# One product for both halves of the keys' operand in an RWKV-7 mixer, with doubled rates

## The chip, the cores and the metric

The kernel runs on one core of a Trainium2 chip. The metric is device time in microseconds (us) of one execution. The core has five engines that run their own instruction queues in order: TensorE (PE, matmuls; its weight loads are shown as PEld), VectorE (DVE), ScalarE (ACT), GpSimd (POOL) and SyncE (SP, which only issues DMAs here).

## The reference, cut to what matters

The whole program is one layer of a latent-token backbone (1024 latent tokens, 256 context tokens, width 1024): a norm, one input projection, three token mixers side by side (RG-LRU, RWKV-7, S5), a gated merge, a SwiGLU and a last norm. The change touches the RWKV-7 mixer alone. It has 8 heads of 64 channels and runs in both directions `d`:

```
w_log = -softplus(-(w0[d] + tanh(wd[:, :, d]) @ w2[d])) - 0.5
decay = exp(-exp(w_log))                       # = exp(-KAPPA * sigmoid(...)), KAPPA = exp(-0.5)
iclr  = sigmoid(a0[d] + ad[:, :, d] @ a2[d])   # the rate a
k_d   = k * (1 + (iclr - 1) * k_a)
s     = s * w_t - (s @ kk_t) (kk_t * a_t) + v_t k_t          # the state, token by token
y     = s @ r_t ;  bonus = sum(r * k_d * r_k) * v
```

The kernel does the scan in chunks of 32 tokens. Within a chunk the keys' operand is divided by the running product of decays: `kk * iclr / P` and `k_d / P`, where 1/P = exp(KAPPA * cum) and `cum` is the running sum of the decays' sigmoids.

## The kernel before, in words

The channels of the mixer come as four pairs of heads (128 partitions). `run` (line 1819) calls `rwkv_pair(p)` for p = 0 to 3, and then the chain over the 40 chunks, `rwkv_chain`, which goes through both directions side by side and must take one chunk after the other. A pair first makes `kk` (a norm with a reciprocal, lines 743 to 749), then goes through 10 groups of 128 tokens, two of the context and eight latent ones. Each group has three parts, one group apart in the loop at line 870:

- `pre` (765 to 783): PE makes the logits of decays and rates for both directions, 512 columns in one PSUM bank: halves `w = 0` (decays) and `w = 1` (rates). ACT takes tanh(x/2) of all 512 (line 777), DVE makes the sigmoid 0.5 t + 0.5 of all 512 (line 778, "the affine") and then two scans over the decays' half (780, 781) into `cum`.
- `mid` (785 to 828): ACT makes `pf` = P (797) and `pi` = 1/P (798). POOL makes t1 = kk * a (807). ACT makes t2 = ka * a + (1 - ka) (808) and POOL multiplies it by k (809). DVE makes `kr` and, in two products, both halves of `kb`: t1 * pi (811) and t2 * pi (812). For latent groups POOL adds the two directions of t2 into `ks` (818), DVE multiplies by r * r_k (819), and PE sums over the channels (821). DVE and ACT then make the gates `glt` (824 to 826).
- `post` (830 to 889): PE multiplies `kb` with `kr` (843), DVE masks the result to `al` (844), ACT copies the square blocks to `aq` (851), PE transposes `kb` (855), ACT copies that to `kt` (856), and SP stores all of it for the chain.

At the end of a pair `aq` is inverted by 60 small products (`rwkv_inverse`, 909 and 911) between two DVE transposes each at the start and the end (904, 905, 913, 914). For pairs 0 to 2 the products run on POOL, under the next pair's groups; for pair 3 and for the context's blocks `aqc` (the first two groups of all pairs) they run on DVE. `aq` has one buffer, so the next pair's first copy to it waits until the inverse has been stored. The auxiliary PSUM tiles of the stage have five buffers, and an `al` holds one until its `aq` copy is done.

PE is filled between these steps with matmuls of other parts of the program (the input projection, line 1302, and the gates' projection, line 1308); `s.fill` hands them out at fixed places of the loop. The order on each engine is set beforehand, by a scheduler that goes through the program with durations of its own; a change of one instruction can so move others.

Of the kernel before, what the change touches and what calls it, by code (L numbers as in the profile page):

```python
# [16 lines left out]
P = 128  # L17
# [604 lines left out]
KAPPA = math.exp(-0.5)  # L622
# [13 lines left out]
class RwkvMixin:  # L636
# [23 lines left out]
    def rwkv_setup(s, pool):  # L660
        nc = s.nc
# [11 lines left out]
        s.tiny = pool.tile([P, 1], F32, name="tiny", tag="tiny")  # L673
        nc.gpsimd.memset(s.tiny, 1e-12)
        s.ka1 = pool.tile([P, 4], F32, name="ka1", tag="ka1")
        nc.vector.tensor_scalar(s.ka1, s.pv("ka"), -1.0, 1.0, op0=ALU.mult, op1=ALU.add)
        s.aqc = pool.tile([P, 32, 32], F32, name="aqc", tag="aqc")
        s.rk_next = None
        s.pf, s.wdt = [], []
# [47 lines left out]
    def rwkv_pair(s, p, pool):  # L727
        nc = s.nc
# [22 lines left out]
        st = {}  # L751
# [13 lines left out]
        def pre(g):  # L765
            sl = slice(P * g, P * g + P)
            wdt = s.wdt[g % 2]
            nc.sync.dma_start(wdt[0:64].rearrange("l k d t -> l (k d) t"),
                              s.wda_d.rearrange("l k d t -> l (k d) t")[:, :, sl])
            ps = s.aux()  # L770
            for w in range(2):
                for d in range(2):
                    o = 256 * w + P * d
                    nc.tensor.matmul(ps[:, o : o + P], w2a[:, w, d], wdt[:, w, d], start=True, stop=True)
            swa = pool.tile([P, 2, 2, P], F32, name="swa", tag="swa", bufs=2)
            sw = swa.rearrange("p w d t -> p (w d t)")
            S.activation(sw, ps, AF.Tanh, scale=0.5)
            V.tensor_scalar(sw, sw, 0.5, 0.5, op0=ALU.mult, op1=ALU.add)
            cum = pool.tile([P, 2, P], F32, name="cum", tag="cum", bufs=2)
            V.tensor_tensor_scan(cum[:, 0], s.smask, swa[:, 0, 0], 0.0, ALU.mult, ALU.add)  # L780
            V.tensor_tensor_scan(cum[:, 1, ::-1], s.smask, swa[:, 0, 1, ::-1], 0.0, ALU.mult, ALU.add)
            pf = s.pf[g % 2]
            st[g] = [swa, cum, pf]

        def mid(g):
# [9 lines left out]
            bc = lambda x: ch(mb(x[:, sl], 2))  # L795
            pi = pool.tile([P, 2, 4, 32], F32, name="pi", tag="pi", bufs=2)
            S.activation(pcur, ch(cum), AF.Exp, scale=-KAPPA)
            S.activation(pi, ch(cum), AF.Exp, scale=KAPPA)
            G.tensor_scalar(s.pcend[:, 0, p, 4 * g : 4 * g + 4], pm[:, 0, :, 32], 1.0, None, op0=ALU.mult)
            G.tensor_scalar(s.pcend[:, 1, p, 4 * g : 4 * g + 4], pm[:, 1, :, 1], 1.0, None, op0=ALU.mult)  # L800
            a4 = ch(swa[:, 1])
            t1 = pool.tile([P, 2, 4, 32], F32, name="t1", tag="t1", bufs=2)
            t2 = pool.tile([P, 2, 4, 32], F32, name="t2", tag="t2", bufs=2)
            kb = pool.tile([P, 4, 2, 64], F32, name="kb", tag="kb", bufs=2)
            kr = pool.tile([P, 2, 4, nr], F32, name="kr", tag="kr", bufs=2)
            kbv = kb.rearrange("p c d x -> p d c x")
            G.tensor_tensor(t1, bc(kk), a4, op=ALU.mult)
            S.activation(t2, a4, AF.Identity, scale=c1("ka"), bias=s.ka1[:, p : p + 1])
            G.tensor_tensor(t2, t2, bc(k), op=ALU.mult)
            V.tensor_tensor(kr[:, :, :, 0:32], bc(kk), pprev, op=ALU.mult)  # L810
            V.tensor_tensor(kbv[:, :, :, 32:64], t1, pi, op=ALU.mult)
            V.tensor_tensor(kbv[:, :, :, 0:32], t2, pi, op=ALU.mult)
            if lat:
                V.tensor_tensor(kr[:, :, :, 32:64], bc(st["r"]), pcur, op=ALU.mult)
                ks = pool.tile([P, P], F32, name="ks", tag="ks", bufs=2)
                vs = pool.tile([P, P], F32, name="vs", tag="vs", bufs=2)
                k2 = t2.rearrange("p d c t -> p d (c t)")
                G.tensor_tensor(ks, k2[:, 0], k2[:, 1], op=ALU.add)
# [1228 lines left out]
```

## Time and profile before

| | us |
|---|---|
| runs | 2295.26, 2298.51, 2294.9 (median 2295.26) |
| profiled execution | 2292.87 |
| its span, first to last instruction | 2291.1 |
| PE busy | 2071.9 (90%) |
| DVE busy | 1623.8 (71%) |
| POOL busy | 1135.8 (50%) |
| ACT busy | 925.9 (40%) |

The span is the time between the first and the last instruction of the profiled execution, and 1.8 us lie around it. "Busy" is an engine's time in instructions; matmuls are pipelined, so a busy PE need not be at its peak. The four pairs lie between 716 and 1126 us of the span, the chain from 1128 to about 1450. The granted clock is a share of full speed of TensorE.

### The profile page before, as it was taken

Reading aid. Unit: us, or ns where it says so; the run is one execution under the profiler, and the core shown is the slowest. Engines: PE = TensorE matmul, PEld = TensorE weight load, DVE = VectorE, ACT = ScalarE, POOL = GpSimd, SP = SyncE. Lnnn points to the kernel's source line nnn. Section 1 sums busy time; section 2 is a strip of 40 time slices with the busy share of each in tenths; the row PEclk is TensorE's granted clock in tenths of the full one; section 3 lists DMA queues with packets and bytes.
Section 4 is the critical chain, followed back from the end, with each engine's and each line's share of the span. In section 5 each row is a group of like instructions: output and inputs, shape, how many; then the busy total and the mean of one; then the engine's idle time right before and its main releaser. Section 6 shows DMA issues by size and latency. Waiting matters only on the chain. (4 is left out here: it accounts for less than half of the span.)

```text
span 2291.1 us, 38462 instructions
## 1 busy us (share of the span) xinstructions
PE 2071.9 (90%) x14441; PEld 1650.5 (72%) x14441; DVE 1623.8 (71%) x2253; ACT 925.9 (40%) x1740; POOL 1135.8 (50%) x1260
## 2 busy tenths in 40 slices
PE   5989978887899988898599999889799999999998
PEld 3868856565778777786467676668588888887786
DVE  5656698889665787889963346853985666568977
ACT  5314345433343646453533433424533232324453
POOL 3662389954522483948100023343564545437656
PEclk7989989998999999999699999999899999999999
DMA  6634322321662635354877768554132323238334
GB/s 258 169 113 114 96 62 76 96 81 60 138 179 75 188 104 156 98 144 122 240 194 165 181 164 210 158 196 152 61 125 92 115 88 120 97 115 298 113 117 153
DMA packets 371751, 314.08 MB, mean 137 GB/s; under 512 B 67239, under 2 KB 313198, under 8 KB 370542
## 3 DMA queue, kind: packets, MB, share of 16 engines
q1 hardware_dynamic: 369134, 304.28, 45.8%
q10 hardware_dynamic: 1728, 6.29, 0.8%
q8 instruction: 114, 1.87, 0.3%
q0 software_dynamic: 704, 1.05, 0.2%
q14 instruction: 71, 0.58, 0.1%
HBM read 217.20 MB, written 94.35 MB: 136 GB/s over the span
## 5 line engine op out<-in xcount | busy, mean ns | idle before, releaser
L1562 PE MATMUL mm<-q,wt 128*128 128x512 f32 x1584 | 376.5, 398 | 4.8 <-DVE q L1476 3.8
L1562 PEld LDWEIGHTS mm<-q,wt 128*128 128x128 f32 x1584 | 299.5, 189 | 77.6 <-DVE q L1476 4.2
L1302 PE MATMUL mm<-xh,wh 128*128 128x512 f32 (+1 forms) x576 | 215.8, 382 | 8.3 <-ACT ya L180 4.8
L1786 PE MATMUL mm<-wt,hk 128*128 128x512 f32 x924 | 218.3, 398 | 5.0 <-DVE hk L1476 4.1
L1302 PE MATMUL mm<-xl,wh 128*128 128x512 f32 (+1 forms) x576 | 215.9, 382 | 1.2 <-DVE xl L1218 1.2
L1786 PEld LDWEIGHTS mm<-wt,hk 128*128 128x128 f32 x924 | 174.5, 189 | 48.7 <-DVE hk L1476 5.5
L1308 PE MATMUL mm<-xh,zh 128*128 128x512 f32 x384 | 161.9, 422 | 9.9 <-ACT zge L1344 5.8
L1308 PE MATMUL mm<-xl,zh 128*128 128x512 f32 x384 | 160.9, 419 | 0.0
L1302 PE MATMUL mm<-xh,wl 128*128 128x512 f32 (+1 forms) x576 | 140.3, 381 | 6.9 <-DVE wl L1295 6.4
L1302 PEld LDWEIGHTS mm<-xh,wh 128*128 128x128 f32 x576 | 115.1, 200 | 28.7 <-ACT ya L180 5.7
L1302 PEld LDWEIGHTS mm<-xl,wh 128*128 128x128 f32 x576 | 114.8, 199 | 19.5 <-DVE xl L1218 1.5
L1308 PE MATMUL mm<-byt,bwh 128*128 128x512 f32 x384 | 118.7, 428 | 7.5 <-DVE bsg L1375 2.2
L1308 PE MATMUL mm<-xh,zl 128*128 128x512 f32 x384 | 110.3, 424 | 14.7 <-DVE zl L1295 14.7
L1302 PEld LDWEIGHTS mm<-xh,wl 128*128 128x128 f32 x576 | 102.4, 196 | 27.8 <-DVE wl L1295 8.1
L1015 DVE TENSOR_TENSOR x<-cg,pcend 64x256 f32<-64x256 f32 x152 | 63.9, 421 | 78.6 <-PE cg L1011 36.0
L1292 POOL CAST bwh<-bwr 128x512 fp32r<-128x512 f32 x16 | 9.9, 617 | 209.2 <-PE mm L1308 111.8
L1475 ACT ACTIVATE wt<-wT 128x512 fp32r<-128x512 f32 x88 | 55.0, 631 | 141.4 <-PE mm L1562 130.3
L1476 DVE TENSOR_TENSOR hk<-hraw,hk 128x512 fp32r<-128x512 f32 x77 | 89.4, 1169 | 24.5 <-ACT hk L1475 24.5
L1268 DVE SCALAR_TENSOR_TENSOR macc<-wm,cs,macc 128x256 f32<-128x256 f32 x112 | 87.1, 777 | 23.0 <-DMA wm<-in_w_mod_dram 20.8
L1308 PEld LDWEIGHTS mm<-xh,zl 128*128 128x128 f32 x384 | 75.1, 201 | 34.3 <-DVE zl L1295 17.5
L1002 ACT ACTIVATE x<-cu 32x256 f32<-32x256 f32 x156 | 58.6, 376 | 101.1 <-PE cu L998 98.0
L1476 DVE TENSOR_TENSOR wt<-wt 128x512 fp32r<-128x512 f32 x70 | 75.2, 1077 | 32.1 <-ACT wt L1475 31.6
(434 smaller groups left out, 5022.5 us busy)
## 6 DMA issues: line engine op xcount, KB each, us to landing
wt<-in_w_ffn_in_dram SPq DMA_DIRECT2D x44, 512.0 KB
hraw<-hidd SPq DMA_DIRECT2D x77, 256.0 KB
hidd<-ft SPq DMA_DIRECT2D x75, 256.0 KB
wm<-in_w_mod_dram SPq DMA_DIRECT2D x64, 256.0 KB
gyl<-gyl SPq DMA_DIRECT2D x32, 512.0 KB
wr<-in_w_in_dram SPq DMA_DIRECT2D x27, 512.0 KB
zr<-in_w_in_dram SPq DMA_DIRECT2D x24, 512.0 KB
sgd<-zge SPq DMA_DIRECT2D x48, 256.0 KB
```

The costliest lines, as they stand in the source:

```text
L1002: S.activation(st["x"][96:128, :, par, :], ps[o : o + 32, 0:256].rearrange("p (a k) -> p a k", a=4), AF.Copy)
L1015: V.tensor_tensor(xn[0:64, :, par, :], sn[r].rearrange("p (a k) -> p a k", a=4), vb(s.pcend[r, d, :, st["c"]], 64), op=ALU.mult)
L1268: nc.vector.scalar_tensor_tensor(acc, wm[:, j], s.cs[:, k + j, 0:1], acc, op0=ALU.mult, op1=ALU.add)
L1292: s.nc.gpsimd.tensor_copy(hi, raw)
L1302: s.nc.tensor.matmul(ps, w(k), a(k), start=n == 0, stop=n == len(seq) - 1)
L1308: s.nc.tensor.matmul(ps, w[:, k], a[:, k], start=n == 0, stop=n == len(seq) - 1)
L1475: s.nc.scalar.activation(hi, raw, AF.Copy)
L1476: (eng or s.nc.vector).tensor_tensor(lo, raw, hi, op=ALU.subtract)
L1562: nc.tensor.matmul(ps, w[:, k], a[:, k], start=n == 0, stop=n == len(seq) - 1)
L1786: nc.tensor.matmul(banks[c % 2][t], a[:, i, P * t : P * t + P], b[:, j], start=c in (0, 1, 3, 5) and k == 0 and q == 0, stop=c in (1, 3, 5 ...
```

## The change

Everything lies in `rwkv_setup`, `pre` and `mid`. The affine step is done for the decays' half alone. The rates stay as the tanh t, with a = (1 + t)/2, so that what is kept is 2a = t + 1, and the missing half goes into the inverse decay: `pi` = exp(KAPPA * cum - ln 2), a bias from a small constant tile. t1 is now t + 1 by ACT (new line 812), then times kk by POOL in place (813). t2 is ka * t + (2 - ka) by ACT, which is twice the old value, then times k by POOL. Both lie in one tile `t12`, 32 tokens of t2 beside 32 of t1, and one DVE product of 512 elements with `pi` repeated makes both halves of `kb` (817). `ks` is twice its old value, and r_k is halved once in the setup. Three small constants are added there, one by DVE and two by POOL.

```diff
-        nc.vector.tensor_scalar(s.ka1, s.pv("ka"), -1.0, 1.0, op0=ALU.mult, op1=ALU.add)
+        nc.vector.tensor_scalar(s.ka1, s.pv("ka"), -1.0, 2.0, op0=ALU.mult, op1=ALU.add)
+        s.rkh = pool.tile([P, 4], F32, name="rkh", tag="rkh")
+        nc.vector.tensor_scalar(s.rkh, s.pv("rk"), 0.5, None, op0=ALU.mult)
+        s.lnh = pool.tile([P, 1], F32, name="lnh", tag="lnh")
+        nc.gpsimd.memset(s.lnh, -math.log(2.0))
+        s.one = pool.tile([P, 1], F32, name="one", tag="one")
+        nc.gpsimd.memset(s.one, 1.0)
...
-            V.tensor_scalar(sw, sw, 0.5, 0.5, op0=ALU.mult, op1=ALU.add)
+            V.tensor_scalar(sw[:, 0:256], sw[:, 0:256], 0.5, 0.5, op0=ALU.mult, op1=ALU.add)
...
-            S.activation(pi, ch(cum), AF.Exp, scale=KAPPA)
+            S.activation(pi, ch(cum), AF.Exp, scale=KAPPA, bias=s.lnh)
...
-            t1 = pool.tile([P, 2, 4, 32], F32, name="t1", tag="t1", bufs=2)
-            t2 = pool.tile([P, 2, 4, 32], F32, name="t2", tag="t2", bufs=2)
+            t12 = pool.tile([P, 2, 4, 2, 32], F32, name="t12", tag="t12", bufs=2)
+            t2, t1 = t12[:, :, :, 0], t12[:, :, :, 1]
...
-            kbv = kb.rearrange("p c d x -> p d c x")
-            G.tensor_tensor(t1, bc(kk), a4, op=ALU.mult)
+            S.activation(t1, a4, AF.Identity, bias=s.one)
+            G.tensor_tensor(t1, t1, bc(kk), op=ALU.mult)
             S.activation(t2, a4, AF.Identity, scale=c1("ka"), bias=s.ka1[:, p : p + 1])
             G.tensor_tensor(t2, t2, bc(k), op=ALU.mult)
             V.tensor_tensor(kr[:, :, :, 0:32], bc(kk), pprev, op=ALU.mult)
-            V.tensor_tensor(kbv[:, :, :, 32:64], t1, pi, op=ALU.mult)
-            V.tensor_tensor(kbv[:, :, :, 0:32], t2, pi, op=ALU.mult)
+            V.tensor_tensor(kb.rearrange("p c d (w x) -> p d c w x", w=2), t12,
+                            pi.unsqueeze(3).to_broadcast([P, 2, 4, 2, 32]), op=ALU.mult)
...
-                V.scalar_tensor_tensor(ks, st["r"][:, sl], c1("rk"), ks, op0=ALU.mult, op1=ALU.mult)
+                V.scalar_tensor_tensor(ks, st["r"][:, sl], s.rkh[:, p : p + 1], ks, op0=ALU.mult, op1=ALU.mult)
```

The lines of the changed kernel are numbered 5 to 6 higher behind the edits. The scheduler puts other instructions in another order too, on all engines within the stage. Three places follow. A number behind a name tells buffers apart; `nt` is the inverse's work tile.

ACT, pair 3, group 7 of the groups 0 to 9, from its tanh (`swa`) to the copies to `aq` that wait for pair 2's inverse. Before:

```order
L777 ACTIVATE swa_9546<-aux_9541 128x512
L808 ACTIVATE t2_9649<-swa_9546,ka1_5208,pv2_1305 128x256
L826 ACTIVATE glt_9575<-aux_9572,pv2_1305 128x128
L797 ACTIVATE pf1_5215<-cum_9549 128x8x32
L798 ACTIVATE pi_9643<-cum_9549 128x256
L851 ACTIVATE aq_8797<-aux_9322 32x128 x4
L851 ACTIVATE aq_8797<-aux_9419 32x128 x4
L851 ACTIVATE aq_8797<-aux_9506 32x128 x4
```

After, first group 7 again, then, one group later, the copies:

```order
L783 ACTIVATE swa_9516<-aux_9511 128x512
L812 ACTIVATE t12_9617<-swa_9516,one_5214 128x8x32
L814 ACTIVATE t12_9617<-swa_9516,ka1_5208,pv2_1305 128x8x32
L831 ACTIVATE glt_9544<-aux_9541,pv2_1305 128x128
L803 ACTIVATE pf1_5221<-cum_9519 128x8x32
L804 ACTIVATE pi_9612<-cum_9519,lnh_5212 128x256
```

```order
L831 ACTIVATE glt_9634<-aux_9631,pv2_1305 128x128
L856 ACTIVATE aq_8773<-aux_9294 32x128 x4
L856 ACTIVATE aq_8773<-aux_9390 32x128 x4
L856 ACTIVATE aq_8773<-aux_9476 32x128 x4
L856 ACTIVATE aq_8773<-aux_9566 32x128 x4
L856 ACTIVATE aq_8773<-aux_9652 32x128 x4
```

The copies of the latent groups 2 to 4 stood behind group 7; now those of groups 2 to 6 stand behind group 8.

DVE, pair 3, the two transposes that end pair 2's inverse (L913 and L914 before, L918 and L919 after) among the context's inverse. Before:

```order
L811 TENSOR_TENSOR kb_9559<-t1_9557,pi_9552 128x2x4x32
L812 TENSOR_TENSOR kb_9559<-t2_9558,pi_9552 128x2x4x32
L913 STREAM_TRANSPOSE aq_7675<-nt_8708 64x32x32
L914 STREAM_TRANSPOSE aq_7675<-nt_8708 64x32x32
L911 TENSOR_TENSOR nt_9201<-nt_9201 128x18x13
L824 TENSOR_TENSOR vs_9569<-aux_9572,zr_8925 128x128
L909 TENSOR_TENSOR nt_9201<-nt_9201 128x238
L778 TENSOR_SCALAR swa_9546<-swa_9546 128x512
```

After:

```order
L916 TENSOR_TENSOR nt_9174<-nt_9174 128x10x21
L817 TENSOR_TENSOR kb_9618<-t12_9617,pi_9612 128x2x4x64
L918 STREAM_TRANSPOSE aq_7661<-nt_8684 64x32x32
L919 STREAM_TRANSPOSE aq_7661<-nt_8684 64x32x32
L914 TENSOR_TENSOR nt_9174<-nt_9174 128x198
L784 TENSOR_SCALAR swa_9606<-swa_9606 128x256
```

The transposes stood behind group 6's `kb`, with group 7's affine behind them; now they stand behind group 7's `kb`, and the context's inverse is eight of its 30 steps further on.

DVE, pair 3, the two transposes that end the context's inverse (`aqc`). Before, they stand behind the last `kb` and the last `al` of the pair:

```order
L1364 SCALAR_TENSOR_TENSOR byt_10070<-byr_10071,byt_10070 128x512
L909 TENSOR_TENSOR nt_9201<-nt_9201 128x30
L844 TENSOR_TENSOR al_9936<-aux_9937,amask_1317 128x512
L911 TENSOR_TENSOR nt_9201<-nt_9201 128x30
L1364 SCALAR_TENSOR_TENSOR byt_10070<-byr_10075,byt_10070 128x512
L913 STREAM_TRANSPOSE aqc_5210<-nt_9201 64x32x32
L914 STREAM_TRANSPOSE aqc_5210<-nt_9201 64x32x32
```

After, group 9's affine, scans, `kr` and `kb` still follow (`byt` is another branch's work):

```order
L918 STREAM_TRANSPOSE aqc_5216<-nt_9174 64x32x32
L919 STREAM_TRANSPOSE aqc_5216<-nt_9174 64x32x32
L784 TENSOR_SCALAR swa_9692<-swa_9692 128x256
L829 TENSOR_TENSOR vs_9714<-aux_9717,zr_8900 128x128
L1369 SCALAR_TENSOR_TENSOR byt_10036<-byr_10037,byt_10036 128x512
L786 SCALAR_TENSOR_TENSOR cum_9695<-smask_5199,swa_9692 128x128
L787 SCALAR_TENSOR_TENSOR cum_9695<-smask_5199,swa_9692 128x128
L1369 SCALAR_TENSOR_TENSOR byt_10036<-byr_10041,byt_10036 128x512
```

So the context's inverse, which the chain's first steps need, now ends a group earlier on DVE, and the last group comes behind it.

## Rows read from the trace of the kernel before

**Rows 1.** Four pairs: us; busy PE, PEld, DVE, ACT, POOL; clock; DMA share; GB/s.

```profile
716.00:804.00 88.00, 82.61 (x729) 70.57 (x728) 74.21 (x120) 54.78 (x124) 37.64 (x62) 1.00 0.56 153
804.00:912.00 108.00, 93.86 (x742) 78.21 (x741) 85.70 (x122) 52.89 (x121) 71.02 (x122) 0.94 0.49 134
912.00:1020.00 108.00, 99.48 (x779) 84.33 (x778) 92.14 (x126) 55.71 (x124) 72.82 (x125) 0.94 0.47 130
1020.00:1126.00 106.00, 78.32 (x635) 64.65 (x633) 99.84 (x180) 49.83 (x119) 65.97 (x111) 0.88 0.55 152
```

**Rows 2.** Waits, 700 to 1170 us: who for whom, us in total, times, longest.

```profile
ACT t L808 <- DVE swa L778: 68.2, 30, 6.5
POOL t L807 <- DVE swa L778: 64.0, 23, 8.1
...
PE aux L821 <- DVE ks L819: 18.6, 9, 4.3
```

**Rows 3.** Single lines (ns min/median/max), then groups by form (busy us, mean ns).

```profile
L778 DVE TENSOR_SCALAR swa<-swa x40: 363/427/1998, 724.7 to 1105.6; 128x512 f32<-128x512 f32 x40
...
L811 DVE TENSOR_TENSOR kb<-t,pi x40: 409/416/869, 733.9 to 1113.2; 128x256 f32<-128x256 f32 x40
...
L812 DVE TENSOR_TENSOR kb<-t,pi x40: 409/419/2114, 734.2 to 1113.6; 128x256 f32<-128x256 f32 x40
...
L812 DVE TENSOR_TENSOR kb<-t,pi 128x256 f32<-128x256 f32 x40 | 25.5, 638 | 0.0
L808 ACT ACTIVATE t<-swa,ka,pv 128x256 f32<-128x256 f32 x40 | 23.9, 599 | 68.5 <-DVE swa L778 68.2
...
L811 DVE TENSOR_TENSOR kb<-t,pi 128x256 f32<-128x256 f32 x40 | 19.7, 492 | 0.2 <-PE aux L855 0.2
...
L798 ACT ACTIVATE pi<-cum 128x256 f32<-128x256 f32 x40 | 16.0, 401 | 0.0
```

**Rows 4.** Groups by form of the nearest other shapes, whole span (the first: 700 to 1180).

```profile
L844 DVE TENSOR_TENSOR al<-aux,amask 128x512 f32<-128x512 f32 x32 | 21.7, 678 | 3.2 <-DMA gyl<-al 2.8 <-PE aux L843 0.4
...
L1364 DVE SCALAR_TENSOR_TENSOR byt<-byr,byt 128x512 fp32r<-128x512 f32 x20 | 14.6, 743 | 6.0 <-ACT byt L1363 5.8
...
L448 DVE TENSOR_SCALAR s<-s 64x128 f32<-64x128 f32 x16 | 3.7, 231 | 2.9 <-PE aux L453 2.8
...
L153 ACT ACTIVATE gi<-aux,lru_hb 128x256 f32<-128x256 f32 x8 | 3.7, 466 | 0.2 <-PE aux L150 0.2
```

**Rows 5.** Busy time of a stretch of 10 us in pair 2, columns as in rows 1.

```profile
950.00:960.00 10.00, 7.93 (x59) 7.07 (x61) 7.34 (x16) 4.21 (x11) 9.69 (x21) 0.66 0.23 55
```

**Rows 6.** Timelines, pair 3: start us, us, instruction, [idle before, who ended it].

```profile
1086.08 0.60 ACT L777 ACTIVATE swa<-aux 128x512 f32<-128x512 f32 x1 [0.24 <-PE aux L774]
...
1089.37 2.13 DVE L914 STREAM_TRANSPOSE aq<-nt 64x1024 f32<-64x1024 f32 x1
...
1092.36 0.42 DVE L778 TENSOR_SCALAR swa<-swa 128x512 f32<-128x512 f32 x1
...
1092.88 0.60 ACT L808 ACTIVATE t<-swa,ka,pv 128x256 f32<-128x256 f32 x1 [6.20 <-DVE swa L778]
...
1092.86 0.73 POOL L807 TENSOR_TENSOR t<-kk,swa 128x256 f32<-128x256 f32 x1 [6.76 <-DVE swa L778]
...
1093.78 0.66 PE L855 MATMUL aux<-ident,kb 128*128 128x128 f32 x4 [2.18 <-ACT glt L826]
1096.98 2.08 PE L774 MATMUL aux<-wdt,w2a 65*128 65x128 f32 x8 [2.54 <-ACT aq L851]
...
1095.81 3.39 ACT L851 ACTIVATE aq<-aux 32x128 f32<-32x128 f32 x12
```

**Rows 7.** Timelines, start of the chain.

```profile
1123.98 1.96 DVE L914 STREAM_TRANSPOSE aqc<-nt 64x1024 f32<-64x1024 f32 x1
...
1128.49 1.07 PE L985 MATMUL mm<-x,gyc 128*32 128x64 f32 x16 [12.63 <-ACT x L929]
1134.03 1.06 PE L998 MATMUL mm<-gs,tt 32*32 32x64 f32 x16 [4.48 <-DMA tt<-ttd]
```

More of the change, by code (lines that the diff above doesn't have):

```diff
@@ L816, in mid @@
                 vs = pool.tile([P, P], F32, name="vs", tag="vs", bufs=2)
-                k2 = t2.rearrange("p d c t -> p d (c t)")
-                G.tensor_tensor(ks, k2[:, 0], k2[:, 1], op=ALU.add)
-                V.scalar_tensor_tensor(ks, st["r"][:, sl], c1("rk"), ks, op0=ALU.mult, op1=ALU.mult)
+                G.tensor_tensor(ks.rearrange("p (c t) -> p c t", c=4), t2[:, 0], t2[:, 1], op=ALU.add)
+                V.scalar_tensor_tensor(ks, st["r"][:, sl], s.rkh[:, p : p + 1], ks, op0=ALU.mult, op1=ALU.mult)
                 ps = s.aux()
```

## The prediction

> **What bounds the kernel now.** Read the windows by stage first, one for each of the four head pairs and one for what follows [rows 1]. The change touches one function that runs 40 times, between 716 and 1126 us, so nothing outside that stage changes cost. In the first three pairs (716 to 1020) PE is busy 82.6, 93.9 and 99.5 us of 88, 108 and 108: 28 us idle in all. DVE is close behind with 74.2, 85.7 and 92.1. ACT is at half. In the fourth pair DVE is busy 99.8 of 106 us and is the bound, while PE falls to 78.3. So the stage has two limits: PE with its filler matmuls in pairs 0 to 2, DVE in pair 3.
>
> Then the waits of the stage [rows 2]. ACT's t2 waits 68.2 us in 30 groups for the affine on DVE (line 778), and POOL's t1 waits 64.0 us for the same instruction. Neither engine is the bound, but both feed `ks`, and PE waits for that nine times, 18.6 us together: its largest wait in the stage.
>
> **The change, part by part.**
> *Affine step halved.* 40 instructions of 512 elements become 256. The row has 363 ns at least and 427 at the median [rows 3]; there is no such row of 256. From below 231 ns (64x128, two dimensions smaller), from above 427 (no gain at all) [rows 3, 4]; I take 300, nearer to the small one since 363 is reached at double the size, so 0.13 us per group, 5 us of DVE over the stage, 0 to 8.
>
> *Two kb products become one of 512.* The pair costs 416 + 419 ns at the median [rows 3]. For one of 512 the nearest rows are the masked product `al` at 678 and the slower `byt` at 743 ns [rows 4]; the new strides and the repeated `pi` are in no row, so the bounds are 0.68 and, as two halves, 0.83. I take 0.69: 0.15 us per group, 6 us in all, 0 to 6. The means are higher, 492 and 638 ns, because single ones take up to 2114 ns while POOL works: 45.2 us busy against 33.4 by medians, so 11.8 us are lost beside POOL. If that loss goes with the time under way, 9.8 us of it stay. The Trainium skill, SBUF — State Buffer, Who interferes with whom, says that a VectorE instruction with two SBUF inputs and a GpSimd one that reads SBUF exclude each other, and that whoever starts first holds on for its whole instruction. By that rule one product is held up once instead of twice, about 6 us would go instead of 2, and DVE's saving over the stage would be 4 us larger; the maximum of 2114 ns agrees with it, no row here tells the two counts apart.
>
> *Together on DVE*: 0.28 us per group, 11 us of 352 in the four pairs, of which only what lies in full stretches counts.
>
> *New on ACT.* t1's step `a+1` on ACT, 256 elements with a pointer bias. The rows for 256 elements are 401 ns without a pointer [rows 3], 466 with one, read from PSUM [rows 4], and 599 with two [rows 3]: 0.40 to 0.60, I take 0.49. The bias on `pi` takes its 401 to about 0.49 too (0.40 to 0.60). That is 0.58 us per group, 23 us on an engine that is busy 213 of 410 us. In front of t2 it lies on the way to `ks`; elsewhere it is hidden by ACT's own waits of 68.2 us, which go. If that cover failed, ten groups of a pair would pay 5.8 us.
>
> *POOL*: t1, t2 and `ks` keep count and size; t1 is now in place and both halves are strided, bounded by 0 and, as one slower 0.1 us in each of 112 instructions, 11 us. I take 0: its work is hidden in pairs 0 and 1 by the 64 us of waits. The three small constants in the setup run once at about 700 us: under 1 us, and PE is full there.
>
> *What the removed wait gives.* ACT and POOL now start from the tanh itself, without DVE's queue. Per group that is 68.2/30 = 2.3 us less 0.5 for the new step: 1.8 us earlier. Of the nine late `ks` three come in windows where POOL is full with the previous pair's inverse and doesn't wait, as at 950 to 960 us with 9.69 of 10 [rows 5]; so six gain, 6 x 1.8 = 11 us at most. PE stops again at the next late operand (weights' low part, `aq`), so I count half: **-5 us** (0 to -11).
>
> *DVE in the starts of pairs 0 to 2.* After each reciprocal DVE is full until about the third group, so 3 groups x 3 pairs x 0.28: **-2 us** (0 to -3).
>
> *Pair 3 and the start of the chain* [rows 6, 7]. Here the order matters. Before, DVE transposes pair 2's inverse until 1091.5, and group 7's affine, though its tanh was done at 1086.7, runs only at 1092.36. ACT's t2 waits 6.20 us, POOL's t1 6.76, and PE waits 2.18 and 2.54 us for `glt` and `aq` queued behind t2. After, group 7 doesn't wait. But the table of the change shows these transposes one group later on DVE, and five `aq` copies instead of three behind them on ACT. I place the transposes at 1094 to 1098 (one group of DVE, about 5 us, ahead of them, less 0.28 x 8 saved), so the copies start near 1101.5, not 1095.8; by then one group more is done. The two shifts cancel about. What doesn't cancel is the end of the context's inverse: before, its last transpose ends at 1125.9, and the second step of the chain waits until 1134.03 for that DMA, 4.48 us after everything else. After, it ends a group earlier on DVE, its store is ahead on SP's queue, and the chain starts from the last kt and the ring's fill alone, so at about 1131: **-3 us** (+6 to -6).
>
> *Behind it* the inverse of pair 3 now stands ahead of more of the chain's products on DVE (15 steps of 0.3 us and two transposes of 2 us in a row). The chain's DVE step may wait 1 to 2 us there: **+1 us** (0 to +2).
>
> **Sum**: -5 - 2 - 3 + 1 = **-9 us**. Against the profiled execution, 2291.1 span plus 1.8 around it, 2292.87 in all, that is 2283.9. The median of the runs is 2.4 above that execution; on its scale 2295.26 - 9 = **2286**.
>
> **Rivals.**
> *Larger gain.* PE's granted clock is 0.94 in pairs 1 and 2 and 0.88 in pair 3, full in pair 0 [rows 1]: it fell below the upper level of 2.4 GHz after PE's idle pieces. 6% of 193 us busy is 12 us. If the six `ks` waits go whole (-11 instead of -5) and half of that clock comes back (-6), the sum is -21, so 2274. For it: the waits are many and short. Against: the other waits (low parts, `aq`) stay.
> *No change.* PE's filler runs in a fixed order; a `ks` that comes earlier only lets PE wait at the next in-order operand. Then only the chain's -3 and +1 remain: 2293. For it: PE is at 91% and DVE at 83% in pairs 0 to 2 [rows 1], so PE has only 28 us to give, spread over many waits.
> *Slower.* The five `aq` copies. PSUM has five auxiliary buffers, and each undelivered `al` holds one. PE cannot go past group 6's kt until the first copy is out. If the transposes come at 1098 and what follows isn't a group shorter, because DVE waits then, the chain starts 5.7 us later (1101.5 instead of 1095.8), with nothing gained in the ks waits: 2295.26 + 5.7 = 2301. It decides from a first copy later than about 1099 on the scale of the profile, if the last kt then comes after 1126.
>
> **How the numbers follow.** About 0.2% (4.6 us) can be told from no change. My forecast (-4.6 to -14) 0.44; larger gain 0.14; no change 0.23; slower 0.19. So faster 0.58, same 0.23, slower 0.19. The range takes the larger gain's centre and the slower rival's: 2272 to 2302; outside lie 0.08 below and 0.12 above. The forecast's own range is 2281 to 2291.
>
> **What would show it.** DVE's affine near 0.3 us, kb near 0.69 in quiet stretches, `pi` and t1 near 0.49. ACT's and POOL's waits for the affine gone; PE's wait for `ks` at a third to two thirds of 18.6; DVE busy in the four pairs down by 9 to 15 us. The chain's second step without a wait for the inverse's DMA, at about 1124 (1134 less 5, 2 and 3). Wrong if PE's idle in pairs 0 to 2 stays near 28, if the wait for the first `aq` grows beyond 6 us, or if the POOL rows grow by more than 0.1 us each.

## The result, and the profile after

The changed kernel took 2309.91 us (median of 5 runs, 2304.96 to 2312.46), against 2295.92 for the kernel before on the same chip: a ratio of 1.0054, 95% interval 1.0042 to 1.0066. It is slower by 0.54%, where 2286 and a range of 2272 to 2302 were forecast. Its profiled execution took 2309.38, with a span of 2307.7. The profiled execution of the kernel before, 2292.87, is 3.1 us faster than that kernel's median here, so by the profiles the loss is 16.6 us, by the medians 14.0.

The stage first, in the four windows of [rows 1], with the same columns: us; busy PE, PEld, DVE, ACT, POOL; clock; DMA share; GB/s.

```profile
716.00:804.00 88.00, 84.46 (x733) 71.89 (x732) 66.52 (x109) 61.21 (x135) 35.52 (x61) 0.98 0.55 151
804.00:912.00 108.00, 97.14 (x781) 81.21 (x781) 81.87 (x114) 62.01 (x138) 73.75 (x125) 0.98 0.49 137
912.00:1020.00 108.00, 95.94 (x765) 80.77 (x764) 83.48 (x114) 60.22 (x134) 75.69 (x123) 0.94 0.45 127
1020.00:1126.00 106.00, 77.90 (x623) 64.83 (x621) 98.48 (x172) 48.76 (x119) 66.94 (x111) 0.82 0.57 156
```

DVE's busy time falls in every pair, 351.9 us to 330.4 in all. PE's busy time hardly moves: 277.5 us in pairs 0 to 2, 275.9 before, so 26.5 us idle where 28.1 were. There DVE was spared 20.2 us, and PE took 1.6 of them. PE's idle time staying near 28 us was one of the prediction's own signs of being wrong.

The single lines (ns min/median/max) that answer to [rows 3]:

```profile
L784 DVE TENSOR_SCALAR swa<-swa x40: 231/294/1060, 727.8 to 1115.0; 128x256 f32<-128x256 f32 x40
...
L817 DVE TENSOR_TENSOR kb<-t,pi x40: 676/686/1190, 735.7 to 1119.6; 128x512 f32<-128x512 f32 x40
...
L812 ACT ACTIVATE t<-swa,one x40: 491/510/512, 721.6 to 1113.5; 128x256 f32<-128x256 f32 x40
...
L804 ACT ACTIVATE pi<-cum,lnh x40: 490/493/528, 734.7 to 1117.6; 128x256 f32<-128x256 f32 x40
```

So the instructions last what was forecast: 294 ns for 300, 686 for 690, 510 and 493 for 490 each. The maximum of the product fell from 2114 to 1190 ns. The waits (who for whom, us in total, times, longest; 700 to 1170 us), against [rows 2]:

```profile
ACT pf L803 <- DVE cum L787: 63.1, 27, 7.5
...
POOL t L813 <- ACT t L812: 59.4, 13, 12.9
...
ACT glt L831 <- DVE glt L830: 39.3, 15, 6.8
...
PE aux L826 <- DVE ks L824: 25.3, 11, 5.8
```

and, from the kernel before, three lines that [rows 2] leaves out:

```profile
ACT pf L797 <- DVE cum L781: 33.0, 33, 3.5
ACT glt L826 <- issue: 21.8, 9, 5.0
...
ACT glt L826 <- DVE glt L825: 14.9, 7, 3.5
```

The waits for the affine are gone, as they had to be, but they came back one step later: ACT now waits for `cum`, which DVE still makes (33.0 us of that in the kernel before, 63.1 now). POOL, which stood 64.0 us in front of t1 for the affine, now stands there 59.4 us for ACT's new step. In front of `glt` little changed: 39.3 us now, and before 14.9 for DVE and 21.8 that the profile puts down to nothing it can see ("issue"), 36.7 in all. PE's wait for `ks` grew from 18.6 to 25.3.

What went wrong stands at the border of pairs 2 and 3. Timeline rows: start us, us, instruction, [idle before, who ended it]. First DVE in the kernel before:

```profile
1016.08 2.02 DVE L904 STREAM_TRANSPOSE nt<-aq 64x1024 f32<-64x1024 f32 x1
1018.12 2.08 DVE L905 STREAM_TRANSPOSE nt<-aq 64x1024 f32<-64x1024 f32 x1
...
1020.23 8.15 DVE L748 RECIPROCAL rn<-rn 128x1280 f32<-128x1280 f32 x1
```

and in the changed kernel:

```profile
1016.02 1.23 DVE L906 TENSOR_TENSOR aq<-aq,imask 128x1024 f32<-128x1024 f32 x1 [1.82 <-ACT aq L856]
1017.31 8.15 DVE L754 RECIPROCAL rn<-rn 128x1280 f32<-128x1280 f32 x1
1025.38 1.95 DVE L909 STREAM_TRANSPOSE nt<-aq 64x1024 f32<-64x1024 f32 x1
1027.34 2.20 DVE L910 STREAM_TRANSPOSE nt<-aq 64x1024 f32<-64x1024 f32 x1
```

Pair 3's reciprocal, 8.15 us long, has passed the two transposes with which the inverse of pair 2 begins. The 60 products of that inverse on POOL wait for them: they start between 1029.6 and 1097.7 where they started between 1020.3 and 1085.6, and their first row says so:

```profile
1029.62 0.35 POOL L914 TENSOR_TENSOR nt<-nt 128x30 f32<-128x30 f32 x1 [2.59 <-DVE nt L910]
```

The inverse is what frees `aq` for pair 3. Its end transposes end at 1102.2 (1091.5 before), and the first `aq` copy of pair 3 starts at 1106.28 (1095.81 before, [rows 6]), with 20 blocks of five groups to copy at once instead of 12 of three:

```profile
1106.28 5.64 ACT L856 ACTIVATE aq<-aux 32x128 f32<-32x128 f32 x20 [1.21 <-DMA ttd<-aq]
```

PE stands three times around these copies, where [rows 6] has 2.18 and 2.54:

```profile
1092.64 1.11 PE L860 MATMUL aux<-ident,kb 128*128 128x128 f32 x4 [3.73 <-ACT glt L831]
...
1105.12 1.98 PE L848 MATMUL aux<-kr,kb 64*64 64x64 f32 x32 [6.35 <-ACT glt L831]
...
1119.10 0.77 PE L826 MATMUL aux<-ks,bones 128*128 128x128 f32 x2 [5.33 <-DVE ks L824]
```

Only the third of these stops comes behind the copies: the tanh of the last group stands on ACT behind them (1112.53), and its affine on DVE 1.9 us more behind the transposes that end the context's inverse (tanh done at 1113.12, affine at 1114.97). The second, 6.35 us, ends with a `glt` that stands on ACT behind `pf` and `pi`, and these wait for a `cum` that DVE makes behind the end transposes of pair 2's inverse (1098.38 to 1102.25). So the late inverse reaches PE in two ways, through DVE's queue and through `aq`.

### The profile page after: what moved, and what is told of

It is laid out like the page before. It is cut to its first block, busy times and chain, and to the rows that moved or that the text cites. A ratio compares the mean times of both kernels' runs of the same rounds, so it can differ in the third digit from the quotient of the medians.

```text
span 2307.7 us, 38479 instructions
## 1 busy us (share of the span) xinstructions
PE 2081.6 (90%) x14441; PEld 1655.6 (72%) x14441; DVE 1595.9 (69%) x2214; ACT 944.0 (41%) x1780; POOL 1142.7 (50%) x1262
## 3 DMA queue, kind: packets, MB, share of 16 engines
q8 instruction: 114, 1.87, 0.3%
## 4 chain that ended last, share of the span: by engine, by line
PE 49%; DVE 18%; POOL 14%; DMA 9%; issue 6%; ACT 4%; SPq 1%; POOLq 0%; DVEq 0%; ACTq 0%
PE mm L1567 18%; PE mm L1307 8%; PE mm L1313 7%; PE mm L1791 4%; PE cg L1016 3%; PE cg L990 2%; PE cu L1003 2%; POOL nt L914 2%; POOL nt L916 2%; DMA wm<-in_w_mod_dram 1%; DVE wt L1481 1%; DVE hk L1481 1%; PE cy L1031 1%; POOL s L214 1%; DVE macc L1273 1%
## 5 line engine op out<-in xcount | busy, mean ns | idle before, releaser
L1007 ACT ACTIVATE x<-cu 32x256 f32<-32x256 f32 x156 | 58.5, 375 | 105.7 <-PE cu L1003 102.8
L1313 PEld LDWEIGHTS mm<-xh,zh 128*128 128x128 f32 x384 | 75.6, 197 | 27.6 <-ACT zge L1349 5.7
```

Source lines behind the costliest of these rows:

```text
L1007: S.activation(st["x"][96:128, :, par, :], ps[o : o + 32, 0:256].rearrange("p (a k) -> p a k", a=4), AF.Copy)
L1313: s.nc.tensor.matmul(ps, w[:, k], a[:, k], start=n == 0, stop=n == len(seq) - 1)
```

## The experiments

Theory: the swap of reciprocal and transposes makes the whole loss, through the late `aq` copies; the new arithmetic by itself costs nothing. The rivals: the arithmetic loses (the merged product, or ACT's and POOL's longer way to `ks`), or the five copies are late for another reason. In the table are all kernels that ran; times are us in each profile. "Last square" is the start of the last product of `kb` with `kr` in pair 3, "chain" the first product `cg<-x,gyc`, "first part" the time from there to the last one of these. Every ratio is against the kernel before on the same chip, from 5 to 12 runs of the kernel and 5 to 35 of the one before. a_recip, b_rev, b_merge and b_rates ran on one chip, the zk kernels and bm_zp on a second, bm_inv6 and the last three on a third. The times are those of one execution each, which can lie some us off the median (bm_inv6: 2310.15, the slowest of its 12 runs, against 2304.5).

| kernel | ratio, 95% | reciprocal, pair 3 | last square | chain | first part |
|---|---|---|---|---|---|
| before | | 1020.2 | 1115.1 | 1138.1 | 52.2 |
| after | 1.0054, 1.0042 to 1.0066 | 1017.3 | 1124.1 | 1143.2 | 58.5 |
| a_recip | 0.9984, 0.9973 to 0.9995 | 1022.5 | 1114.0 | 1140.5 | 51.0 |
| b_rev | 1.0054, 1.0037 to 1.0070 | 1022.1 | 1131.5 | 1151.7 | 50.7 |
| b_merge | 1.0052, 1.0037 to 1.0067 | 1033.3 | 1130.6 | 1148.1 | 54.5 |
| b_rates | 0.9978, 0.9963 to 0.9993 | 1020.4 | 1114.6 | 1140.2 | 49.9 |
| a_zk | 1.0014, 1.0003 to 1.0024 | 1015.6 | 1112.0 | 1140.3 | 59.6 |
| a_recip_zk | 1.0041, 1.0025 to 1.0057 | 1024.0 | 1114.8 | 1139.2 | 67.0 |
| b_zk | 1.0056, 1.0035 to 1.0076 | 1025.4 | 1120.0 | 1143.4 | 65.4 |
| bm_zp | 1.0031, 1.0020 to 1.0043 | 1031.2 | 1128.0 | 1150.5 | 52.1 |
| bm_inv6 | 1.0024, 1.0012 to 1.0037 | 1028.0 | 1124.6 | 1147.7 | 52.0 |
| a_i3 | 0.9993, 0.9980 to 1.0007 | 1016.7 | 1122.9 | 1142.7 | 49.6 |
| a_recip_i3 | 0.9998, 0.9984 to 1.0013 | 1020.3 | 1113.4 | 1137.2 | 52.2 |
| a_recip_inv6 | 1.0004, 0.9993 to 1.0016 | 1020.8 | 1114.3 | 1135.8 | 53.6 |

### The swap undone: a_recip

The changed kernel with one more edge for the scheduler: pair 3's reciprocal is issued after the transposes.

```diff
-        V.reciprocal(rn, rn)
+        if p == 3:
+            with s.tc.issue_after(s.invt.ins):
+                V.reciprocal(rn, rn)
+        else:
+            V.reciprocal(rn, rn)
...
-        V.transpose(tu(nt[b]), tu(aq[b]))
+        s.invt = V.transpose(tu(nt[b]), tu(aq[b]))
```

> The changed kernel with one edge added: on DVE, pair 3's reciprocal (8.15 us) stands behind the first two transposes of pair 2's inverse again, as in the kernel before. Theory (order): this one swap starts the inverse on POOL 9.3 us later (1029.6 instead of 1020.3), its last transposes come at 1098 instead of 1087, the first copy to aq at 1106.3 instead of 1095.8, and that costs the 12 us lost in the last 30 us of pair 3 and the 6 us behind it in the chain. Undone, the inverse starts near 1017, the copies start before 1097, and the time is 2309.9 less 12 to 18, so 2292 to 2298. Rival (arithmetic): the new step on ACT and the strided products on POOL cost the time, and the place of the reciprocal is a side effect: 2305 to 2312. Rival (chain): the start of the chain costs it (its inverse of the context and first loads): about 2309.9 less 6, 2302 to 2306.

The rows of DVE, then ACT's first copy for pair 3:

```profile
1018.18 1.98 DVE L913 STREAM_TRANSPOSE nt<-aq 64x1024 f32<-64x1024 f32 x1
1020.18 2.24 DVE L914 STREAM_TRANSPOSE nt<-aq 64x1024 f32<-64x1024 f32 x1
...
1022.46 8.15 DVE L756 RECIPROCAL rn<-rn 128x1280 f32<-128x1280 f32 x1
...
1095.48 3.39 ACT L860 ACTIVATE aq<-aux 32x128 f32<-32x128 f32 x12
```

Three groups of copies at 1095.48, as before, and 0.9984: one edge turns the loss of 0.54% into a gain of 0.16%. The arithmetic by itself is not what loses.

### The swap alone: b_rev

The kernel before, its arithmetic untouched; only pair 3's head (k, kk and the reciprocal) is written ahead of pair 2's inverse, and the transposes are issued after the reciprocal.

```diff
+        if p == 2:
+            s.head = s.rwkv_head(3, pool)
-        o = s.rwkv_inverse(aq, s.invp, "nt", nc.vector if INV[p] else nc.gpsimd)
+        o = s.rwkv_inverse(aq, s.invp, "nt", nc.vector if INV[p] else nc.gpsimd, s.recip if p == 2 else None)
...
+            with s.tc.issue_after(late.ins):
+                V.transpose(nt[f], tu(aq[f]))
+                V.transpose(tu(nt[b]), tu(aq[b]))
```

> The kernel before, arithmetic untouched, with the swap alone: pair 3's reciprocal ahead of the first two transposes of pair 2's inverse on DVE. The scheduler then puts the five aq copies behind group 8 and the context's last transposes ahead of group 9, as in the changed kernel. Theory (order): inverse on POOL starts 9 us later, first aq copy near 1106 to 1109, time 2295.9 plus 12 to 18: 2306 to 2314. Rival (arithmetic): the swap is harmless since POOL has 37 us of waits in pair 3: 2293 to 2299. Rival (chain): only the context's earlier inverse and the loads at the chain's start matter: 2296 to 2302.

Reciprocal, the first product of the inverse, the first copy, and PE's last `ks` in front of the end of the pair:

```profile
1022.13 8.15 DVE L748 RECIPROCAL rn<-rn 128x1280 f32<-128x1280 f32 x1 [3.21 <-ACT rn L747]
...
1034.50 0.49 POOL L925 TENSOR_TENSOR nt<-nt 128x30 f32<-128x30 f32 x1 [2.20 <-DVE nt L921]
...
1112.02 5.66 ACT L860 ACTIVATE aq<-aux 32x128 f32<-32x128 f32 x20 [1.12 <-DMA ttd<-aq]
...
1126.59 0.77 PE L830 MATMUL aux<-ks,bones 128*128 128x128 f32 x2 [6.40 <-DVE ks L828]
```

The old arithmetic with the swap loses 0.54%, the whole loss of the changed kernel, and shows the same five copies. Its reciprocal also waits for ACT's square roots, and so the copies are later still, at 1112. That the two ratios are equal is therefore in part chance: the inverse starts 14.2 us later than in the kernel before, in the changed kernel 9.3, while the chain's first part, 6.3 us longer in the changed kernel, is no longer here than before (50.7 against 52.2).

### The two halves of the change: b_rates and b_merge

b_rates is the kernel before with the affine for the decays alone, t1 on ACT and the doubled rates, but still two products for `kb` (the constants `ka1`, `rkh`, `lnh` and `one` as in the change). b_merge is the kernel before with the one product and the full affine.

```diff
(b_rates)
-            V.tensor_scalar(sw, sw, 0.5, 0.5, op0=ALU.mult, op1=ALU.add)
+            V.tensor_scalar(sw[:, 0:256], sw[:, 0:256], 0.5, 0.5, op0=ALU.mult, op1=ALU.add)
...
-            S.activation(pi, ch(cum), AF.Exp, scale=KAPPA)
+            S.activation(pi, ch(cum), AF.Exp, scale=KAPPA, bias=s.lnh)
...
-            G.tensor_tensor(t1, bc(kk), a4, op=ALU.mult)
+            S.activation(t1, a4, AF.Identity, bias=s.one)
+            G.tensor_tensor(t1, t1, bc(kk), op=ALU.mult)
...
(b_merge)
...
-            V.tensor_tensor(kbv[:, :, :, 32:64], t1, pi, op=ALU.mult)
-            V.tensor_tensor(kbv[:, :, :, 0:32], t2, pi, op=ALU.mult)
+            V.tensor_tensor(kb.rearrange("p c d (w x) -> p d c w x", w=2), t12,
+                            pi.unsqueeze(3).to_broadcast([P, 2, 4, 2, 32]), op=ALU.mult)
```

> The kernel before with the other half of the change: affine step for the decays alone, t1's step on ACT, doubled rates and halved inverse decay; two products of 256 for kb. The scheduler keeps the reciprocal behind the transposes here. Theory (order): the earlier t1 and t2 gain up to 6 us as pairs 0 to 2 did in the changed kernel: 2289 to 2297. Rival (arithmetic, ACT step): with the 40 new steps the loss is here, 2303 to 2312.

> The kernel before with one half of the change: t1 and t2 in one tile and one product of 512 for kb; affine step whole, no step on ACT, rates not doubled. The scheduler keeps the reciprocal behind the transposes here. Theory (order): a small gain of DVE time alone, 0.15 to 0.2 us in 40 groups, of which a part counts: 2290 to 2297. Rival (arithmetic, ACT step): also 2290 to 2297, as it has no new step. Rival (POOL's strided writes cost): 2297 to 2303.

b_rates gains 0.22%, and its reciprocal stands behind the transposes. a_recip has the merged product in the same order of work; the two ratios differ by 0.0006, with intervals of 0.0011 and 0.0015 to each side, so no gain of the merged product can be told. b_merge loses as much as the whole change, which neither its theory nor its rivals had, and yet it does not have the swap. Its copies for pair 2 wait for the store of pair 1's inverse, and then ACT stands at a split `zh` of the projection's weights in front of the last two, which start 13 us later than the last two of the kernel before (1011.57 and 1013.68):

```profile
996.16 4.52 ACT L849 ACTIVATE aq<-aux 32x128 f32<-32x128 f32 x16 [6.96 <-DMA ttd<-aq]
...
1023.74 1.06 ACT L1292 ACTIVATE zh<-zr 128x1024 fp32r<-128x1024 f32 x1 [3.24 <-DMA zr<-in_w_in_dram]
1024.81 1.11 ACT L849 ACTIVATE aq<-aux 32x128 f32<-32x128 f32 x4
1026.66 1.11 ACT L849 ACTIVATE aq<-aux 32x128 f32<-32x128 f32 x4
```

So pair 3's reciprocal comes at 1033.3, and from there on everything is late. It is again `aq` between two pairs that comes late, by another placement.

### Two repairs of b_merge: bm_zp and bm_inv6

bm_zp casts the split of that one weight block on POOL instead of ACT; bm_inv6 issues t1 of group 6 of pair 2 behind the last product of pair 1's inverse on POOL, so that this inverse ends sooner.

```diff
(bm_zp)
-            hi, lo = s.wsplit(s.i["w_in"][0][:, P * (27 + i) : P * (28 + i)], KD, s.fp, "z", 1, 2, 1)
+            hi, lo = s.wsplit(s.i["w_in"][0][:, P * (27 + i) : P * (28 + i)], KD, s.fp, "z", 1, 2, 1, i == 22)
(bm_inv6)
+            if p == 2 and g == 6:
+                with s.tc.issue_after(s.invl.ins):
+                    G.tensor_tensor(t1, bc(kk), a4, op=ALU.mult)
+            else:
+                G.tensor_tensor(t1, bc(kk), a4, op=ALU.mult)
```

> The one-product half of the change (b_merge) once more, with one weight split (the 23rd of the gates' projection) made by POOL instead of ACT. In b_merge it stood on ACT ahead of pair 2's last two aq copies and waited there for its DMA until 1023.7, so the reciprocal came at 1033.3 instead of 1020.2. Theory (order): the reciprocal comes back to 1020 to 1024 and the time to 2293 to 2300. Rival (the product of 512 or the strided tile costs the 12 us): 2305 to 2312.

> The one-product half of the change (b_merge) with the same edge in pair 2. In b_merge the copies of pair 2 waited 6.96 us for the store of pair 1's inverse, seven steps of which stood on POOL behind groups 6 and 7, and pair 3's reciprocal came 13 us later than before. Theory (that order makes b_merge's loss): reciprocal back from 1033 to 1022 to 1026, time 2295 to 2302. Rival (the product of 512 costs it): 2305 to 2312.

Each gives back a part, 0.2 and 0.3%, little more than the intervals, and neither the whole. The reciprocal comes back only to 1031.2 and 1028.0. In bm_inv6 the wait of 6.96 us for the store falls to 1.93 (first row), in bm_zp it stays at 7.25 (second):

```profile
994.16 4.52 ACT L853 ACTIVATE aq<-aux 32x128 f32<-32x128 f32 x16 [1.93 <-DMA ttd<-aq]
...
998.07 4.52 ACT L849 ACTIVATE aq<-aux 32x128 f32<-32x128 f32 x16 [7.25 <-DMA ttd<-aq]
```

So both delays seem to have a part in b_merge's loss; what is left of it, 0.2 to 0.3%, stays open.

### The swap kept, `aq` not shared: a_zk, b_zk, a_recip_zk

If the late `aq` is the way by which the swap costs time, then a buffer of its own for pair 3 must remove the delay although the swap stays. It takes a second buffer of the shifted keys (`zk`), which is free in pair 3. The same edit was made in the kernel before (b_zk) and in a_recip (a_recip_zk), for what it costs by itself.

```diff
-        aq = s.invp.tile([P, 32, 32], F32, name="aq", tag="aq")
+        if p < 3:
+            aq = s.invp.tile([P, 32, 32], F32, name="aq", tag="aq")
+        else:
+            aq = pool.tile([P, NT], F32, name="zk", tag="zk", bufs=2)[:, 0:1024].rearrange("p (a c) -> p a c", c=32)
```

> The changed kernel, swap kept (pair 3's reciprocal ahead of the transposes of pair 2's inverse), but pair 3's aq lies in a buffer of its own (a zk buffer that is free by then), so that its copies wait for no inverse; each aq copy then stands behind its own group on ACT. Theory (late inverse holds the aq copies, these hold PSUM's auxiliary tiles and ACT): the loss goes although the swap stays: 2309.9 less 12 to 18, 2292 to 2298, and pair 3's last square products end near 1115 instead of 1124. Rival (the swap costs by itself, through the later keys' operand and POOL's fuller groups): 2303 to 2312.

> The kernel before with pair 3's aq in its own buffer and nothing else. Theory (copies): PE's waits of 2.18 and 2.54 us at group 7 shrink: 2290 to 2296. Rival (DVE bound): 2294 to 2299. Against the changed kernel with the same buffer it gives what the changed arithmetic is worth where the order can't put the copies late.

> The changed kernel with both: reciprocal behind the transposes, and pair 3's aq in its own buffer. Theory (aq copies are what pair 3 waits for): the 4 us that PE waits at the copies even with the reciprocal in place go too: 2286 to 2294. Rival (with the copies out of the way DVE is the bound of pair 3, 98 of 106 us busy): as with the edge alone, 2292 to 2298.

In a_zk the reciprocal still stands ahead (1015.6), POOL's inverse still starts late (1028.0), and yet pair 3's last square product stands at 1112.0, 12 us earlier than in the changed kernel and 3 earlier than before. That shows that pair 3's delay hangs on the shared `aq`. DVE's order moved with the edit, too (the transposes that end the context's inverse now stand behind the last group, 1114.98 to 1118.87), and the two were not parted. The total did not follow in full: 1.0014, and the two companions lose 0.56 and 0.57% by the edit. The windows of the chain's first part tell why, a_zk's two and then b_zk's (columns as in [rows 1]):

```profile
1140.30:1179.30 39.00, 34.77 (x532) 29.39 (x531) 26.55 (x61) 14.99 (x38) 0.61 (x1) 0.50 0.71 189
1179.30:1199.90 20.60, 20.60 (x158) 15.63 (x159) 7.27 (x13) 1.99 (x6) 1.97 (x3) 0.93 0.75 191
...
1143.40:1189.20 45.80, 40.58 (x562) 33.24 (x560) 30.79 (x72) 15.85 (x40) 1.07 (x2) 0.50 0.62 163
```

The branch's filler products (`mm<-byt,bwh`) now begin at 1179.27 in a_zk and 1189.23 in b_zk, instead of 1145.27 in the changed kernel and 1147.24 in the one before. Until then PE runs the chain's small products at a granted clock of 0.50, the lower level of 1.2 GHz. That the filler waits for the room of the longer held `zk` is argued from the order of times: SP issues the first load of its weights (`bwr`) at 1170.58 in a_zk, 1179.07 in b_zk and 1178.24 in a_recip_zk instead of 1139.70 in the changed kernel, each time behind the end of pair 3's inverse, which now lies in `zk` (1164.36, 1172.04 and 1167.85). That the edit itself costs the time, b_zk shows, against its expectation. So b_zk and a_recip_zk take 65 to 67 us for a part that takes 52 and 51 without the edit.

### The inverse of pair 3 on POOL: a_i3, a_recip_i3

The changed kernel loses 9.0 us at the last square product but 11.4 at the end of the chain's first part. 4 us are regained at the chain's start (+5.1), and 6.3 lost in that part. A DVE busy with pair 3's inverse was the suspect. `INV` chooses the engine of each inverse (1 is DVE):

```diff
-INV = (0, 0, 0, 1, 1)
+INV = (0, 0, 0, 0, 1)
```

> The changed kernel, swap kept, with pair 3's inverse on POOL instead of DVE (nothing else moves up to the end of pair 3). In the changed kernel the chain's product on DVE stood behind this inverse: PE idle 1.87 us at 1154 and 2.09 us at 1170, granted clock 0.50 from 1154 to 1163, and the first part of the chain 6.3 us longer than before. Theory (that queue on DVE makes the chain's share of the loss): these two stops go and the first part of the chain shrinks from 58.4 to about 52 us, time 2303 to 2306, with pair 3's share still lost. Rival (the clock is low anyway after pair 3's idle stretch): 2308 to 2312. Rival (POOL now converts the branch's weights too late for the chain's filler): 2312 to 2320.

> The changed kernel with the reciprocal behind the transposes and pair 3's inverse on POOL. Theory (both shares of the loss undone, DVE free in the chain): first part of the chain at or below 51 us, 2290 to 2295. Rival (POOL's weight conversions for the branch come later and the filler runs dry): 2296 to 2306.

In the changed kernel, PE and DVE in the chain:

```profile
1153.72 0.43 DVE L1020 TENSOR_TENSOR x<-cg,pcend 64x256 f32<-64x256 f32 x1
...
1154.25 1.07 PE L990 MATMUL cg<-x,gyc 128*32 128x64 f32 x16 [1.87 <-issue]
...
1165.70 1.98 DVE L918 STREAM_TRANSPOSE aq<-nt 64x1024 f32<-64x1024 f32 x1
1167.69 2.02 DVE L919 STREAM_TRANSPOSE aq<-nt 64x1024 f32<-64x1024 f32 x1
1169.74 0.88 DVE L1020 TENSOR_TENSOR x<-cg,pcend 64x256 f32<-64x256 f32 x2
...
1170.72 1.00 PE L990 MATMUL cg<-x,gyc 128*32 128x64 f32 x16 [2.09 <-issue]
```

The profile puts the 1.87 and 2.09 us down to "issue", that is to nothing it can see; but PE starts 0.1 us after DVE's `x` ends each time, and the second `x` stood behind two transposes of 2 us. The windows there, the changed kernel's first and then a_i3's:

```profile
1154.00:1163.00 9.00, 8.75 (x78) 6.45 (x79) 8.30 (x23) 1.50 (x4) 0.00 (x0) 0.50 0.33 81
1163.00:1172.00 9.00, 6.91 (x105) 4.83 (x104) 8.59 (x18) 2.06 (x6) 0.61 (x1) 0.88 0.34 104
...
1154.00:1192.30 38.30, 35.55 (x552) 25.22 (x550) 16.81 (x28) 11.53 (x31) 17.05 (x34) 1.00 0.64 173
```

DVE at 8.3 and 8.6 of 9 us, and a clock of 0.50 for 9 us after PE had waited; on POOL the same inverse leaves DVE at 17 of 38 and the clock at 1.00. The first part takes 49.6 instead of 58.5 us, and the time is 0.9993, better than the 2303 to 2306 expected, although pair 3's last square product is still at 1122.9 and its first `aq` copy at 1104.96. This limits the theory: of the 7.9 us that pair 3 is late in a_i3, 0.9 are left at the end of the chain's second part (1448.6, before 1447.8), so the late copies cost the whole time only together with pair 3's inverse on DVE. Whether that inverse on POOL would gain in the kernel before as well was not run. With the swap undone as well (a_recip_i3), pair 3 ends 9.5 us earlier, but the time is 0.9998, no better than a_recip's 0.9984: the two repairs do not add. What takes the second one back was not settled; the last product of the chain's second part (`cg<-x,gyl`) starts at 1453.6 there, at 1448.6 in a_i3 and at 1451.1 in a_recip.

### A better placement still: a_recip_inv6

a_recip with bm_inv6's edge as well.

```diff
+            if p == 2 and g == 6:
+                with s.tc.issue_after(s.invl.ins):
+                    G.tensor_tensor(t1, t1, bc(kk), op=ALU.mult)
```

> The changed kernel with the reciprocal behind the transposes, and in pair 2 POOL's t1 of group 6 behind the last product of pair 1's inverse, so that the aq copies of pair 2, which waited 5.03 us for that inverse's store, start earlier (near 983 instead of 989.6). Theory (the one aq buffer is what pair 2 waits for as well): 2 to 5 us less than with the first edge alone: 2289 to 2293. Rival (group 6 comes later by what the copies win): 2293 to 2300.

Pair 2's first copy starts at 987.28, not at 983 (989.64 in a_recip). The reciprocal comes 1.6 us earlier than in a_recip and the chain 4.7, but the last square product does not, the chain's first part is 2.6 us longer, and 1.0004 is no gain. The best kernels that ran are b_rates and a_recip, which both beat the kernel before, by 0.2%, and the changed one.

## Why the prediction was wrong

**The step that failed** is the one on pair 3, "Here the order matters". It saw that the end transposes stand one group later on DVE and that five copies instead of three stand behind them. But it took that for a move on DVE of one group, which would cost no time, and wrote "The two shifts cancel about". The end transposes come later because their inverse starts later, 9.3 us, behind the reciprocal, and nothing in the later groups could cancel that: from pair 2's masking to its last square product pair 3 took 108.0 us instead of 100.2. It forecast the transposes at 1094 to 1098 and the copies near 1101.5; they end at 1102.2, and the copies start at 1106.28. Only the place where the chain of 60 products ends was read, never where it starts. The swap itself was to be seen in the order of the two kernels, at the start of pair 3.

Why the scheduler swapped is argued, not shown: it takes what is ready, and pair 3's square roots on ACT now stand partly ahead of pair 2's last `aq` copy, so the reciprocal is ready before the transposes are. Either half of the change alone keeps them ahead.

**The rival "Slower"** had the right mechanism, late copies and PE held behind them, and its condition came true: a first copy at 1106.28 and a last `kt` at 1126.62, where 1099 and 1126 were its limits. Its price was too small, 5.7 us against 16.6 us of span. These have four parts, by the milestones of the two profiles: +5.1 at the chain's start, +6.3 in the chain's first part, +1.3 in its second (last product at 1460.5 instead of 1447.8, 12.7 later), and +3.9 behind it. Not all of this is the change's: 3.1 us lie already ahead of pair 0's reciprocal (719.74, before 716.64), and with the old arithmetic b_merge, b_rev and b_zk have 717.49, 719.39 and 722.41 there. Of the 3.9 us 2.5 are one group of 96 filler products (`mm<-wt,q`), which took 22.65 us from 1511.38 before and 25.10 us from 1523.84 after, with the same wait of 2.27 us ahead of it and a granted clock of 1.00 before and 0.89 after. Why the clock was lower there is not known.

**-5 for the `ks` waits** did not come: they grew from 18.6 to 25.3, and in pairs 0 to 2 alone from 12.3 to 14.5. Without the swap (a_recip) they are 17.8 in all, so some 7 us of the 25.3 are the swap's, and of the forecast 5 to 11 there is hardly anything. The rival "No change" had this, that an earlier operand lets its engine wait for the next one. From the end of the tanh to the start of t2 it is 26.0 us in all 40 groups, where it was 132.7, but to `cum`, on the same DVE, it is 188.8, where it was 191.4, and `kb` needs `pi` and so `cum`. Which of the late operands keeps `ks` itself late is not shown.

**-2 for DVE after the reciprocals** cannot be told apart from this, but the sum of both can. From pair 0's reciprocal to pair 2's masking the changed kernel takes 296.3 us, a_recip 296.5, b_rates 295.1, the kernel before 298.2. All kernels with either arithmetic whole and nothing edited in pairs 0 to 2 agree with this: 296.0 to 296.5 with the new one (six kernels), 297.7 to 298.3 with the old one (three). So about 2 us were gained, of 7.

**-3 at the chain's start** was right in its cause and worth nothing. The 4.48 us for the inverse's transfer [rows 7] are gone, but the first step itself comes 4.3 us later (1132.77, before 1128.49), and the third step has a new wait:

```profile
1132.77 1.07 PE L990 MATMUL mm<-x,gyc 128*32 128x64 f32 x16 [7.89 <-ACT x L934]
1134.52 1.06 PE L1003 MATMUL mm<-gs,tt 32*32 32x64 f32 x16 [0.69 <-ACT gs L994]
...
1140.05 1.06 PE L990 MATMUL mm<-x,gyc 128*32 128x64 f32 x16 [4.47 <-DMA x<-vd]
```

ACT fills the ring `x` behind the last `kt` (at 1127.20, before at 1121.89), so the second step came at 1134.52, not at 1124, and the third waits 4.47 us for the next transfer.

**+1 for pair 3's inverse on DVE** (0 to +2) had the mechanism and not the size: the two waits alone are 4.0 us, and the clock fell with them. a_i3 shortens the part by 8.9.

**Prices of instructions** were right, all four, as durations. DVE's saving in the four pairs was 21.5 us instead of 11. `kb`'s durations fell by 13.4 (45.2 us of [rows 3] to 31.8): 6.0 by the medians, as forecast, and 7.4 of what DVE lost beside POOL, where I had let 2 go. But a duration is more than what the engine gives up: back to back, DVE starts an instruction some 0.08 us before the last one ends. Two products start at 933.58 and 933.92 in the kernel before and the next at 934.25, 0.67 us for the two; the one product starts at 1006.36 and the next instruction at 1006.96, 0.60 us. So in quiet stretches merging gives back 0.07 us per group and not 0.15, 2.8 us in 40 groups and not 6. By form (busy us, mean ns; idle before), the changed kernel's product, and b_rates' two in the same order of work:

```profile
L817 DVE TENSOR_TENSOR kb<-t,pi 128x512 f32<-128x512 f32 x40 | 31.8, 796 | 0.6 <-POOL t L815 0.6
...
L819 DVE TENSOR_TENSOR kb<-t,pi 128x256 f32<-128x256 f32 x40 | 22.9, 571 | 0.0
...
L818 DVE TENSOR_TENSOR kb<-t,pi 128x256 f32<-128x256 f32 x40 | 20.2, 504 | 0.0
```

40 products at the median of 686 ns are 27.4 us, so 4.4 are lost beside POOL; by the medians of [rows 3] b_rates' two lose 9.7 (43.1 less 33.4), those of [rows 3] 11.8. I had kept 9.8, and 4 us of DVE's saving hung on that. So somewhat more than half of the loss went. The Trainium skill, SBUF — State Buffer, Who interferes with whom, lets such a DVE product and a GpSimd read exclude each other, and this agrees with the estimate drawn from it, that one product is held up once instead of twice, against the choice I made; no run separates that from the time under way. It bought little: the 20.2 us that DVE was spared in pairs 0 to 2 came with about 2 us.

## What to carry to other kernels

Where a scheduler sets the order, look at what a change moves at the start of every long chain on another engine, not only at its end: here one instruction of 8.15 us in front of two transposes of 2 us delayed 60 products, and with them a shared buffer, five copies and the next stage. A half that tells nothing alone can turn the order together with the other, so a change is worth measuring with the order held (one edge gave 0.70% here) before its arithmetic is judged. Busy time saved on an engine that feeds others is worth only what the next late operand allows: 20 us of DVE in pairs 0 to 2 bought about 2.

## What the runs showed of the hardware

TensorE's granted clock stayed low through long stretches in which PE was busy for some nine tenths of the time. In a_zk PE was busy 34.77 of 39.00 us with the chain's small products at a granted clock of 0.50, the level of 1.2 GHz, and in b_zk 40.58 of 45.80 us; in a_zk it was 0.93 in the stretch after, when the filler products had begun. The prediction had put the clock's fall down to PE's idle pieces alone. In b_zk and a_recip_zk, where the filler came late at the chain's start, the first part took 13 to 16 us longer (65.4 and 67.0 us beside 52.2 and 51.0), more than the 6.3 that it lost in the changed kernel; in a_zk it took 1.2 us longer than there.
